# A seven-product step at the head of three matrix calls in a feed-forward layer

## The chip, the cores and the metric

The kernel runs on one core of a Trainium2 chip. The metric is the time of one execution on the device, in microseconds (us); the median of a few runs is given. The engines are TensorE (PE; its weight loads are shown as PEld), VectorE (DVE), ScalarE (ACT), GpSimd (POOL) and SyncE (SP, which here only issues DMAs). Everything is in float32.

## The reference

Two layers over 256 tokens of width 2048, each a mixer and a feed-forward part, with a normalisation before each and a last one behind:

```python
def rms_norm(x, g):
    y = x * lax.rsqrt(jnp.mean(x * x, axis=-1, keepdims=True) + EPS)
    return y * g

def sq_relu_mlp(h, w1, w2):          # w1: 2048 x 8192, w2: 8192 x 2048
    return jnp.square(jax.nn.relu(h @ w1)) @ w2

def reference(x, ...):
    x = x + neighbourhood_attention(rms_norm(x, na_norm), na_wqkv, na_rpb, na_wo)
    x = x + sq_relu_mlp(rms_norm(x, ffn0_norm), ffn0_w1, ffn0_w2)
    x = x + dilated_attention(rms_norm(x, dil_norm), dil_wqkv, dil_wo)
    x = x + sq_relu_mlp(rms_norm(x, ffn1_norm), ffn1_w1, ffn1_w2)
    return rms_norm(x, final_norm)
```

The change lies in `sq_relu_mlp`, at its first matrix, w1 ("first matrices" of the two layers).

## The kernel before

**Matrix products in parts.** A float32 operand is kept as a rounded part (hi, type float32r) and the residue (lo). A product is three matmuls: hi·hi, hi·lo, lo·hi (`three`, L199 to L201), each 128 x 128 against 128 x 512. ScalarE casts to hi and VectorE subtracts for lo (`split`, L194 and L195: `wh` and `wl` for the weights).

**The feed-forward part** works in four groups of 2048 hidden columns. Each group has four calls of `gemm_pair`: two with w1 (`cp` 0 and 1, 1024 columns each), then two with w2. A call makes a block of 256 x 1024 results: 2 x 2 blocks of 128 tokens x 512 columns. It has eight steps, one for each "pair", 256 rows of the weights: a 2 x 2 block product of 2 x 2 blocks. A plain step ("s") does eight products, 24 matmuls. An "x" step does the same work with seven products of sums of blocks (the Strassen-Winograd scheme), 21 matmuls: it needs sums of the activations' blocks (S1 to S4, made once: `sums_and_parts`) and sums of the weights' blocks (made in each step: `prep_x`). With w1 pairs 2, 4 and 6 are "x" in each call (`FF_PAIRS`), so the steps are s s x s x s x s; with w2 the order is s s x s x s x s too, except in the last group.

**Banks.** All eight banks of PSUM are one tile. A call uses four for the plain blocks, called "2", "4", "S" and "3", and four for the extra products, "1", "6", "7", "5". Call by call they change places (`sum_banks`): the banks of "1", "6", "7", "5" are those in which the call before had "2", "4", "S", "3", and the other way round. A plain step's products come in the order "2", "4", "S", "3" (two products in each); a seven-product step's in the order of `X`: "1", "2", "6", "7", "4", "3", "5".

At the end of a call its banks are emptied, in the course of its last step: `begin` (L350 and after: the banks "1", "6", "7", "5" become C, a copy on ScalarE and three instructions on VectorE), then, for w2, `put` adds each of "2", "4", "S", "3" to x, one after each quarter of the step; for w1, `last_sum`. A part of C is added to x some steps later (`early`). After a call with w1 the results are transposed into spare banks in the second step of the next call.

**The order of the work is written out by hand.** The main loop goes through the steps. In step i TensorE gets the step's products in four quarters. Between them the loop issues, in this order within a quarter: transposes, what hangs on the quarter (`s.after`: begin, put, last_sum, sums of activations), and then a part of `prep(i + 2, n)`, which makes the weights' parts for the step after next. At its end stand `prep(i + 2, 3)` and `load(i + 5)`, the weights' DMA on SP. Each engine works through its queue in that order. `prep` of a plain step is two splits of half a tile (128 x 1024). `prep_x` is: three adds on VectorE (a fourth sum among them) at n = 0; a split of one half and the cast of the sums (`hs`, L180) at n = 1; the residue of the sums (`ls`) at n = 2; a split of the other half at n = 3. Four halves have buffers (`hlpool`, 4), the sums one (`sums`), their parts two (`hs`, `ls`), the weights three (`wpool`).

**The norm** ahead of a feed-forward part (`Norm`) transposes x block by block into spare banks and makes hi and lo of the activations. Of a pair in `FF_PAIRS` it keeps S1 in the place of the block A21, and S3, S2, S4 in a tile of its own (`xs`).

Of the kernel before, what the change touches and what calls it, by code (L numbers as in the profile page):

```python
# [48 lines left out]
def tile_encoder(ctx: ExitStack, tc: tile.TileContext, ins, out):  # L49
# [41 lines left out]
    def scratch(shape, name):  # L91

        if part.name[0] == "f":
            return part.pool.tile(shape, F32, name=name, tag="t", bufs=2)
        return part.pool.tile(shape, F32, name=name, tag="p", bufs=5)

    class Banks:
# [36 lines left out]
    def subtract(engine, out, a, b):  # L134
        engine.tensor_tensor(out=out, in0=a, in1=b, op=ALU.subtract)  # L135
# [156 lines left out]
    def gemm_pair(w, cp, A, sums_of, order, finish, split_end=False, soon=False):  # L292
        made, q = [], {}
        first_x = [n for n, o in enumerate(order) if o[0] == "x"]
        touched = set()

        def left(pair, which):

            t, u = A[pair // 2], 2 * (pair % 2)
            if which in ("S2", "S3", "S4"):  # L300
                c = sums_of[pair]
                return [c[:, h, ("S3", "S2", "S4").index(which), :] for h in range(2)]
            a, ts_ = {"A11": (0, 0), "A12": (1, 0), "S1": (0, 1), "A21": (0, 1), "A22": (1, 1)}[which]
            return [t[:, u + a, h, ts_ * P:(ts_ + 1) * P] for h in range(2)]

        def product(bank, a, b, last):
            if not q:
                q.update({k: banks[:, n, :] for k, n in sum_banks().items()})
            three(q[bank], a, b, bank not in touched, last)
            touched.add(bank)  # L310

        X = (("1", "A11", 2), ("2", "A12", 3), ("6", "S2", 6), ("7", "S3", 4), ("4", "A22", 0), ("3", "S4", 1),
             ("5", "S1", 5))

        for n, (kind, pair) in enumerate(order):
            k, u = pair // 2, pair % 2
            loads = [(w[k, 2 * cp + c].rearrange("p (a n) -> p a n", n=512)[:, 2 * u:2 * u + 2, :],
                      2 - 2 * c, 4 - 2 * c) for c in (1, 0)]
            if kind == "x":
                def quarter(s, m, pair=pair, n=n):  # L320
                    for bank, a, b in X[2 * m:2 * m + 2]:
                        product(bank, left(pair, a), (s.hi[b], s.lo[b]), n == first_x[-1] and bank in "1567")
            else:
                def quarter(s, m, pair=pair, n=n):
                    tb, c = QUARTERS[m]
                    for kk in range(2):
                        b = 2 * (1 - c) + kk
                        a = (("A11", "A12"), ("A21", "A22"))[tb][kk]
                        product(STD[tb, c], left(pair, a), (s.hi[b], s.lo[b]), n == len(order) - 1 and kk == 1)
            s = Step(kind, loads, quarter)  # L330
            s.even = pair % 2 == 0
            steps.append(s)
            made.append(s)

        if split_end:
            ends = made[-2:]
            for e, s in enumerate(ends):
                def quarter(s, m, e=e):
                    tb, m = m // 2, m % 2
                    pair = order[len(order) - 2 + m][1]  # L340
                    for kk in range(2):
                        b = 2 * (1 - e) + kk
                        a = (("A11", "A12"), ("A21", "A22"))[tb][kk]
                        product(STD[tb, e], left(pair, a), (ends[m].hi[b], ends[m].lo[b]), m == 1 and kk == 1)
                s.quarters = quarter

        def begin(m):
            if m == 0:
                C = q["C"] = part.pool.tile([P, 4, 512], F32, name="C", tag="C")
                nc.scalar.copy(C[:, 0, :], q["1"])  # L350
                subtract(nc.vector, C[:, 1, :], q["6"], C[:, 0, :])
            elif m == 1:
                subtract(nc.vector, q["C"][:, 2, :], q["C"][:, 1, :], q["7"])
            elif m == 2:
                add(nc.vector, q["C"][:, 1::2, :], q["C"][:, 1:3, :], q["5"].unsqueeze(1).to_broadcast([P, 2, 512]))

        s = made[first_x[-1] + 1]
        for m in range(3):
            s.after[0 if s is made[-1] else min(m, 1) if soon else m].append(lambda m=m: begin(m))
        finish(made, q)  # L360
        return made
# [8 lines left out]


    class Norm:
        def __init__(self, n, perm, pairs=()):
            self.n, self.perm = n, perm
            self.pairs, self.sums = pairs, {}
            self.xT = [None] * NB
            self.ss = small.tile([P, 2, NB], F32, name="ss", tag="ss", bufs=2)
# [14 lines left out]
        def parts(self, c, half):  # L392
# [1 line left out]
                self.xT[c] = xpool.tile([P, 4, 2, T], F32R, name="xT", tag="xT")  # L394
            xT = self.xT[c]
            if 2 * c + half in self.pairs:
                raw = scratch([P, 2, T], "gx")
                for a in range(2):
                    k = 4 * c + 2 * half + a
                    nc.scalar.activation(raw[:, a, :], self.tp[:, a, :], AF.Copy, scale=gT[:, self.n, k:k + 1])  # L400
                self.sums[2 * c + half] = part.pool.tile([P, 2, 3, P], F32R, name="xs", tag="xs", bufs=len(self.pairs))
                sums_and_parts(raw, xT, half, self.sums[2 * c + half])
                return
            for which, a in [(which, 2 * half + a) for which in ("hi", "lo") for a in range(2)]:
# [46 lines left out]
            self.r = small.tile([P, 2], F32, name="rstd", tag="rstd", bufs=2)  # L451
            nc.vector.tensor_copy(self.r, self.r_ps[:, 0, 0:4].rearrange("p (t u) -> p t u", u=2)[:, :, 0])

    def sums_and_parts(raw, t, half, sums):

        c = scratch([P, 3, P], "c")
        a11, a21, a12, a22 = raw[:, 0, :P], raw[:, 0, P:], raw[:, 1, :P], raw[:, 1, P:]
        subtract(nc.vector, c[:, 0, :], a11, a21)
        subtract(nc.vector, a21, a21, a22)
        subtract(nc.vector, c[:, 1, :], a11, a21)  # L460
        subtract(nc.vector, c[:, 2, :], a12, c[:, 1, :])
        hi, lo = (t[:, 2 * half:2 * half + 2, h, :] for h in range(2))
        nc.scalar.copy(hi, raw)
        nc.scalar.copy(sums[:, 0], c)
        subtract(nc.vector, lo, raw, hi.bitcast(F32))
        subtract(nc.vector, sums[:, 1], c, sums[:, 0].bitcast(F32))

    def rsqrt_mean(ss):

# [188 lines left out]
    def out_rows(w, xT, nk, norm, chunk_done, order, late_block=None):  # L658
        accs = [{} for _ in range(NB)]
        for c, k in order:  # L660
            made = gemm_rows(w, c * 512, xT, [k], accs[c], 0, nk - 1)
            if k == nk - 1:
                add_rows(made, c, accs[c], norm, chunk_done, late_block)

    def begin_norm(n, perm, pairs=()):
        norms[n] = Norm(n, perm, pairs)
        return pending_norm(lambda: norms[n], n == 2)

    FF_PAIRS = (2, 4, 6)

    def ff_order(pairs, order=range(8)):
        return [("x" if k in pairs else "s", k) for k in order]

    parts = {len(steps) + 9: "feed-forward"}
    out_rows(ins["na_wo"], na_oT, 4, lambda: norms[1], begin_norm(1, False, FF_PAIRS),
             [(c, k) for c in range(3) for k in range(3)] + [(c, 3) for c in range(3)] + [(3, k) for k in range(4)], 2)


    def ffn(norm, w1, w2, next_norm, next_done):
        for g in range(4):  # L680
# [4 lines left out]
            def hidden(made, q, cp, hT=hT, sums=sums, pairs2=pairs2, last=last):  # L685
# [14 lines left out]
                for r in range(4):  # L700
# [10 lines left out]
                    def post(r=r, held=held):  # L711
                        c, half, pair = 2 * cp + r // 2, r % 2, 4 * cp + r
                        if half == 0:
                            hT[c] = opool.tile([P, 4, 2, T], F32R, name="hT", tag="o")
                        if pair in pairs2:
                            raw = part.pool.tile([P, 2, T], F32, name="h", tag="h", bufs=2)
                            nc.scalar.copy(raw, held["t"])
# [9 lines left out]
                    at(i + 1, pe, post, quarter=r)  # L727

            for cp in range(2):
                gemm_pair(w1, 2 * g + cp, norm.xT, norm.sums, ff_order(FF_PAIRS), lambda made, q, cp=cp: hidden(made, q, cp))  # L730

            w2g = w2[4 * g:4 * (g + 1)]

# [188 lines left out]
    for hh in range(2):  # L922
# [16 lines left out]
        for h in range(4):  # L939
# [2 lines left out]
               quarter=(1, 3)[h % 2])  # L942

    parts[len(steps) + 2] = "feed-forward"
    out_rows(ins["dil_wo"], dil_oT, 2, lambda: norms[3], begin_norm(3, False, FF_PAIRS),
             [(0, 0), (1, 0), (0, 1), (1, 1), (2, 0), (2, 1), (3, 0), (3, 1)])


# [210 lines left out]
```

## Time and profile before

| | |
|---|---|
| median of 3 runs | 2255.3 us (2255.12 to 2255.54) |
| the profiled execution | 2256.32 us |
| its span, first to last instruction | 2254.5 us |
| mean granted TensorE clock | 0.998 |
| first feed-forward part, its steps | 398.6 to about 1081 us |
| second feed-forward part | 1562.6 to about 2240 us |
| first steps of groups two to four | 569.95, 739.67, 909.37 and 1733.91, 1903.60, 2073.30 us |

How its lines are read: a row of the timeline is "start, duration, engine, line, operation, output <- inputs, shapes, count [idle time before it <- what ended it]". The durations of consecutive instructions of VectorE overlap a little, so that the spacing of their starts is the time they take in the queue: a 128 x 1024 residue has 1.22 us and takes 1.14. A row of the waits is "who <- for whom: us in total, times, longest". A row of the windows is "stretch, its length, busy time (and count) of PE, PEld, DVE, ACT and POOL, granted clock, busy share of the DMA engines, GB/s". A row of the groups of instructions ends in "busy us, mean ns of one | idle before".

### The profile page before, as it was taken

What the parts mean: (1) busy time and instruction counts of PE and PEld (TensorE: products, weight loads), DVE (VectorE), ACT (ScalarE), POOL (GpSimd) and SP (SyncE); (2) the same over time, 40 slices, a digit from 0 to 9 for tenths busy, and PEclk for the clock granted to TensorE, in tenths of its full rate; (3) what the DMA queues carried; (4) which work ended last, traced back from release to release, by engine and by line L of the source; (5) the groups of instructions that cost most, each with busy time, mean ns of one, the idle gap of its engine ahead of it and who ended that gap; (6) DMA issues with size and microseconds to landing.
All of it is one profiled execution on the core that took longest, in us unless ns stands there. A gap on an engine that the chain in (4) does not pass through costs nothing.

```text
span 2254.5 us, 28417 instructions
## 1 busy us (share of the span) xinstructions
PE 2241.5 (99%) x10924; PEld 1888.4 (84%) x10924; DVE 1871.7 (83%) x2215; ACT 1261.0 (56%) x1570; POOL 0.7 (0%) x6
## 2 busy tenths in 40 slices
PE   9999999999999999999999999999999999999998
PEld 8888888888888888888888888888888888888886
DVE  6776666899899999989877667757999999999988
ACT  6454455665565565565544544456665665665664
POOL 0000000000000000000000000000000000000000
PEclk9999999999999999999999999999999999999999
DMA  7556555556656656655555445444666666666664
GB/s 250 180 183 197 174 180 180 190 187 206 204 187 204 205 189 200 204 180 189 211 182 184 174 168 181 175 168 150 207 206 194 197 203 195 200 193 202 203 216 138
DMA packets 110728, 430.33 MB, mean 191 GB/s; under 512 B 23872, under 2 KB 24448, under 8 KB 92160
## 3 DMA queue, kind: packets, MB, share of 16 engines
q1 hardware_dynamic: 109920, 426.82, 57.9%
q8 instruction: 85, 1.39, 0.2%
q10 hardware_dynamic: 672, 1.70, 0.2%
q14 instruction: 51, 0.42, 0.1%
HBM read 426.38 MB, written 2.10 MB: 190 GB/s over the span
## 4 chain that ended last, share of the span: by engine, by line
PE 97%; DVE 1%; ACT 1%; issue 1%; DMA 0%; ACTq 0%; POOLq 0%; POOL 0%; DVEq 0%
PE banks L200 25%; PE banks L201 25%; PE banks L199 25%; PE banks L228 13%; PE banks L233 7%; PE banks L708 1%; PE banks L390 0%; DMA w<-in_na_wqkv_dram 0%; PE banks L906 0%; PE banks L866 0%; PE banks L603 0%; ACT junk L382 0%; DVE wl L195 0%; ACT wh L194 0%; DVE sums L138 0%
## 5 line engine op out<-in xcount | busy, mean ns | idle before, releaser
L195 DVE TENSOR_TENSOR wl<-w,wh 128x1024 fp32r<-128x1024 f32 (+1 forms) x802 | 965.1, 1218 | 254.4 <-ACT wh L194 165.9
L194 ACT CAST wh<-w 128x1024 fp32r<-128x1024 f32 (+1 forms) x802 | 828.2, 1048 | 496.4 <-PE banks L201 338.2
L199 PE MATMUL banks<-wh,xT 128*128 128x512 f32 x1104 | 434.9, 394 | 0.0
L200 PE MATMUL banks<-wl,xT 128*128 128x512 f32 x1104 | 430.1, 390 | 0.5 <-DVE wl L195 0.5
L201 PE MATMUL banks<-wh,xT 128*128 128x512 f32 x1104 | 430.1, 390 | 0.0
L199 PE MATMUL banks<-wh,hT 128*128 128x512 f32 x804 | 316.2, 393 | 0.0
L228 PE MATMUL banks<-xT,wh 128*128 128x512 f32 x1280 | 312.8, 393 | 1.1 <-DVE xT L421 1.1
L201 PE MATMUL banks<-wh,hT 128*128 128x512 f32 x804 | 313.2, 390 | 0.0
L200 PE MATMUL banks<-wl,hT 128*128 128x512 f32 x804 | 312.9, 389 | 0.0
L228 PEld LDWEIGHTS banks<-xT,wh 128*128 128x128 f32 x1280 | 233.4, 189 | 46.2 <-DVE xT L421 1.3
L201 PEld LDWEIGHTS banks<-wh,xT 128*128 128x128 f32 x1104 | 207.3, 188 | 43.5
L200 PEld LDWEIGHTS banks<-wl,xT 128*128 128x128 f32 x1104 | 207.6, 188 | 41.9 <-DVE wl L195 1.4
L199 PEld LDWEIGHTS banks<-wh,xT 128*128 128x128 f32 x1104 | 207.5, 188 | 40.8
L180 ACT CAST hs<-sums 128x1536 fp32r<-128x1536 f32 x92 | 136.4, 1483 | 159.9 <-DVE sums L138 159.9
L201 PEld LDWEIGHTS banks<-wh,hT 128*128 128x128 f32 x804 | 150.9, 188 | 31.7
L199 PEld LDWEIGHTS banks<-wh,hT 128*128 128x128 f32 x804 | 151.0, 188 | 30.1
L200 PEld LDWEIGHTS banks<-wl,hT 128*128 128x128 f32 x804 | 151.1, 188 | 30.0
L233 PE MATMUL banks<-xT,wl 128*128 128x256 f32 x1280 | 172.7, 284 | 0.0
L233 PEld LDWEIGHTS banks<-xT,wl 128*128 128x128 f32 x1280 | 165.8, 191 | 6.4 <-DVE wl L195 0.2
L135 DVE TENSOR_TENSOR ls<-sums,hs 128x1536 fp32r<-128x1536 f32 x92 | 161.2, 1752 | 10.7 <-ACT hs L180 10.7
L138 DVE TENSOR_TENSOR sums<-w 128x1024 f32<-128x1024 f32 x92 | 112.1, 1219 | 0.0
L199 PE MATMUL banks<-wh,oT 128*128 128x512 f32 x192 | 76.6, 399 | 0.0
(190 smaller groups left out, 2298.2 us busy)
## 6 DMA issues: line engine op xcount, KB each, us to landing
w<-in_ffn_w_dram SPq DMA_DIRECT2D x512, 512.0 KB, 4.7
w<-in_dil_wqkv_dram SPq DMA_DIRECT2D x72, 1024.0 KB, 4.8
w<-in_na_wqkv_dram SPq DMA_DIRECT2D x47, 1024.0 KB, 5.1
w<-in_na_wo_dram SPq DMA_DIRECT2D x16, 1024.0 KB, 4.8
w<-in_dil_wo_dram SPq DMA_DIRECT2D x8, 1024.0 KB, 4.8
bias<-in_rpb_dram SPq DMA_DIRECT2D x32, 96.0 KB, 9.9
out_dram<-x SPq DMA_DIRECT2D x8, 256.0 KB, 2.6
x<-in_x_dram SPq DMA_DIRECT2D x3, 512.0 KB, 9.3
```

What stands on the lines that cost most here:

```text
L135: engine.tensor_tensor(out=out, in0=a, in1=b, op=ALU.subtract)
L138: engine.tensor_tensor(out=out, in0=a, in1=b, op=ALU.add)
L180: nc.scalar.copy(s.hs, s.sums)
L194: nc.scalar.copy(dst_hi, src)
L195: nc.vector.tensor_tensor(out=dst_lo, in0=src, in1=dst_hi.bitcast(F32), op=ALU.subtract)
L199: nc.tensor.matmul(o, left[0], right[0], start=start, stop=False)
L200: nc.tensor.matmul(o, left[0], right[1], start=False, stop=False)
L201: nc.tensor.matmul(o, left[1], right[0], start=False, stop=stop)
L228: nc.tensor.matmul(acc[j // 2][:, j % 2, :], s.hi[a][:, j * P:(j + 1) * P], xT[k][:, a].rearrange("p h t -> p (h t)"), start=k == 0 and a ...
L233: nc.tensor.matmul(acc[j // 2][:, j % 2, :T], s.lo[a][:, j * P:(j + 1) * P], xT[k][:, a, 0, :], start=False, stop=k == nk - 1 and a == 3)
L708: nc.tensor.transpose(t[:, a, tb * P:(tb + 1) * P], q["C"][:, 2 * tb + f // 4, f % 4 * P:(f % 4 + 1) * P], ident)
```

## The change

In groups two to four the first call with w1 has pair 0 as a seven-product step too: x s x s x s x s. The second call with w1, and group one, keep pair 0 plain; so for pair 0 the norm keeps A21 and makes four sums (`FF_KEPT`, tile `xk`). With this the sums are made in a tile of seven blocks (`blocks`: three sums, four own blocks), in which two of the four small subtractions are one instruction, and the norms' scratch tiles share its two buffers ("h").

```diff
     def scratch(shape, name):
         if part.name[0] == "f":
-            return part.pool.tile(shape, F32, name=name, tag="t", bufs=2)
+            return part.pool.tile(shape, F32, name=name, tag="h", bufs=2)
...
-            if which in ("S2", "S3", "S4"):
+            names = ("S3", "S2", "S4", "S1")[:sums_of[pair].shape[2]] if pair in sums_of else ()
+            if which in names:
                 c = sums_of[pair]
-                return [c[:, h, ("S3", "S2", "S4").index(which), :] for h in range(2)]
+                return [c[:, h, names.index(which), :] for h in range(2)]
...
             if 2 * c + half in self.pairs:
-                raw = scratch([P, 2, T], "gx")
+                keep = int(2 * c + half in self.kept)
+                raw = blocks()
...
-    def sums_and_parts(raw, t, half, sums):
-
-        c = scratch([P, 3, P], "c")
-        a11, a21, a12, a22 = raw[:, 0, :P], raw[:, 0, P:], raw[:, 1, :P], raw[:, 1, P:]
-        subtract(nc.vector, c[:, 0, :], a11, a21)
-        subtract(nc.vector, a21, a21, a22)
-        subtract(nc.vector, c[:, 1, :], a11, a21)
-        subtract(nc.vector, c[:, 2, :], a12, c[:, 1, :])
-        hi, lo = (t[:, 2 * half:2 * half + 2, h, :] for h in range(2))
-        nc.scalar.copy(hi, raw)
-        nc.scalar.copy(sums[:, 0], c)
-        subtract(nc.vector, lo, raw, hi.bitcast(F32))
-        subtract(nc.vector, sums[:, 1], c, sums[:, 0].bitcast(F32))
+    def blocks():
+        return part.pool.tile([P, 7, P], F32, name="h", tag="h", bufs=2)
+
+    def sums_and_parts(b, t, half, sums):
+        hi, lo = (t[:, 2 * half:2 * half + 2, h, :].rearrange("p a (u t) -> p a u t", u=2) for h in range(2))
+        whole = b[:, 3:7, :].rearrange("p (a u) t -> p a u t", u=2)
+        keep = sums.shape[2] == 4
+        def own():
+            nc.scalar.copy(hi, whole)
+            subtract(nc.vector, lo, whole, hi.bitcast(F32))
+        if keep:
+            own()
+        subtract(nc.vector, b[:, 0:5:4, :], b[:, 3:5, :], b[:, 4:7:2, :])
+        subtract(nc.vector, b[:, 1, :], b[:, 3, :], b[:, 4, :])
+        subtract(nc.vector, b[:, 2, :], b[:, 5, :], b[:, 1, :])
+        if not keep:
+            nc.scalar.copy(hi, whole)
+        for n, src in ((slice(0, 3), b[:, 0:3, :]), (slice(3, 4), b[:, 4:5, :]))[:1 + keep]:
+            nc.scalar.copy(sums[:, 0, n], src)
+        if not keep:
+            subtract(nc.vector, lo, whole, hi.bitcast(F32))
+        for n, src in ((slice(0, 3), b[:, 0:3, :]), (slice(3, 4), b[:, 4:5, :]))[:1 + keep]:
+            subtract(nc.vector, sums[:, 1, n], src, sums[:, 0, n].bitcast(F32))
...
-    FF_PAIRS = (2, 4, 6)
+    FF_PAIRS, FF_KEPT = (2, 4, 6), (0,)
...
             for cp in range(2):
-                gemm_pair(w1, 2 * g + cp, norm.xT, norm.sums, ff_order(FF_PAIRS), lambda made, q, cp=cp: hidden(made, q, cp))
+                gemm_pair(w1, 2 * g + cp, norm.xT, norm.sums, ff_order(FF_PAIRS + (FF_KEPT if g and not cp else ())), lambda made, q, cp=cp: hidden(made, q, cp))
```

More of the change, by code (lines that the diff above doesn't have):

```diff
@@ L372, in tile_encoder, with __init__ @@
     class Norm:
-        def __init__(self, n, perm, pairs=()):
-            self.n, self.perm = n, perm
+        def __init__(self, n, perm, pairs=(), kept=()):
+            self.n, self.perm, self.kept = n, perm, kept
             self.pairs, self.sums = pairs, {}
@@ L396, in parts @@
             if 2 * c + half in self.pairs:
-                raw = scratch([P, 2, T], "gx")
+                keep = int(2 * c + half in self.kept)
+                raw = blocks()
                 for a in range(2):
                     k = 4 * c + 2 * half + a
-                    nc.scalar.activation(raw[:, a, :], self.tp[:, a, :], AF.Copy, scale=gT[:, self.n, k:k + 1])
-                self.sums[2 * c + half] = part.pool.tile([P, 2, 3, P], F32R, name="xs", tag="xs", bufs=len(self.pairs))
+                    nc.scalar.activation(raw[:, 3 + 2 * a:5 + 2 * a, :].rearrange("p u t -> p (u t)"), self.tp[:, a, :], AF.Copy, scale=gT[:, self.n, k:k + 1])
+                self.sums[2 * c + half] = part.pool.tile([P, 2, 3 + keep, P], F32R, name="xs", tag=("xs", "xk")[keep],
+                                                              bufs=1 if keep else len(self.pairs) - len(self.kept))
                 sums_and_parts(raw, xT, half, self.sums[2 * c + half])
@@ L663, in out_rows, with begin_norm @@
                 add_rows(made, c, accs[c], norm, chunk_done, late_block)
-    def begin_norm(n, perm, pairs=()):
-        norms[n] = Norm(n, perm, pairs)
+    def begin_norm(n, perm, pairs=(), kept=()):
+        norms[n] = Norm(n, perm, pairs + kept, kept)
         return pending_norm(lambda: norms[n], n == 2)
-    FF_PAIRS = (2, 4, 6)
+    FF_PAIRS, FF_KEPT = (2, 4, 6), (0,)
     def ff_order(pairs, order=range(8)):
@@ L674, in tile_encoder @@
     parts = {len(steps) + 9: "feed-forward"}
-    out_rows(ins["na_wo"], na_oT, 4, lambda: norms[1], begin_norm(1, False, FF_PAIRS),
+    out_rows(ins["na_wo"], na_oT, 4, lambda: norms[1], begin_norm(1, False, FF_PAIRS, FF_KEPT),
              [(c, k) for c in range(3) for k in range(3)] + [(c, 3) for c in range(3)] + [(3, k) for k in range(4)], 2)
@@ L715, in post @@
                         if pair in pairs2:
-                            raw = part.pool.tile([P, 2, T], F32, name="h", tag="h", bufs=2)
-                            nc.scalar.copy(raw, held["t"])
+                            raw = blocks()
+                            nc.scalar.copy(raw[:, 3:7, :].rearrange("p (a u) t -> p a (u t)", u=2), held["t"])
                             def parts_of(c=c, half=half, raw=raw, pair=pair):
@@ L944, in tile_encoder @@
     parts[len(steps) + 2] = "feed-forward"
-    out_rows(ins["dil_wo"], dil_oT, 2, lambda: norms[3], begin_norm(3, False, FF_PAIRS),
+    out_rows(ins["dil_wo"], dil_oT, 2, lambda: norms[3], begin_norm(3, False, FF_PAIRS, FF_KEPT),
              [(0, 0), (1, 0), (0, 1), (1, 1), (2, 0), (2, 1), (3, 0), (3, 1)])
```

## The prediction

> **What bounds the kernel now.** I read the page first: the span, the engines' busy time, and the chain that ended last.
>
> ```profile
> span 2254.5 us, 28417 instructions
> PE 2241.5 (99%) x10924; PEld 1888.4 (84%) x10924; DVE 1871.7 (83%) x2215; ACT 1261.0 (56%) x1570; POOL 0.7 (0%) x6
> ...
> PE 97%; DVE 1%; ACT 1%; issue 1%; DMA 0%; ACTq 0%; POOLq 0%; POOL 0%; DVEq 0%
> ```
>
> TensorE sets the end: 97% of the chain. A matmul taken away counts in full, as long as nothing makes TensorE wait. So next the waits, and then the busy times over one whole group of the first feed-forward layer (group two, 569.95 to 739.67 us).
>
> ```profile
> ACT wh L194 <- PE banks L201: 338.2, 253, 3.2
> PEld banks L200 <- DVE wl L195: 1.4, 2, 0.7
> PEld banks L199 <- DVE hT L195: 1.3, 8, 0.2
> ...
> 569.95:739.67 169.72, 169.72 (x766) 140.52 (x764) 158.40 (x170) 101.22 (x110) 0.00 (x0) 1.00 0.62 199
> ```
>
> ScalarE's casts wait for TensorE (338.2 us, for a free buffer), while TensorE's own waits in the feed-forward part are of the order of 1 us in all. One of them matters here: eight times a weight load waited for VectorE to empty a bank (hT L195). In the group TensorE is busy for all of its 169.72 us, but VectorE for 158.40 of them, 93%. It has 11 us to spare per group, and where in the group they lie decides this case.
>
> The price of the two kinds of step is read from TensorE's timeline at the border between group one and group two (the first matmuls of the last two steps of group one, and of the first step of group two).
>
> ```profile
> 559.75 0.39 PE L199 MATMUL banks<-wh,hT 128*128 128x512 f32 x1
> ...
> 564.51 0.39 PE L199 MATMUL banks<-wh,hT 128*128 128x512 f32 x1
> ...
> 569.95 0.39 PE L199 MATMUL banks<-wh,xT 128*128 128x512 f32 x1
> ...
> 569.72 0.19 PEld L199 LDWEIGHTS banks<-wh,xT 128*128 128x128 f32 x1
> ```
>
> A step of seven products takes 564.51 - 559.75 = 4.76 us (21 matmuls), one of eight 569.95 - 564.51 = 5.44 us (24 matmuls): 0.227 us a matmul. The first weight load of the step that the change turns into seven products starts at 569.72.
>
> **The change part by part.**
>
> *TensorE.* Six steps (three groups in two layers) go from 24 to 21 matmuls: 6 x 0.68 = 4.1 us less.
>
> *VectorE and ScalarE at the border.* The new step, called x0 here, needs sums of weights: it is prepared like other seven-product steps. Its preparation is issued during the step of 559.75, ahead of the emptying of that call's banks. VectorE's and ScalarE's queues there:
>
> ```profile
> 550.88 1.23 DVE L195 TENSOR_TENSOR wl<-w,wh 128x1024 fp32r<-128x1024 f32 x1 [0.18 <-ACT wh L194]
> 552.02 1.22 DVE L138 TENSOR_TENSOR sums<-w 128x1024 f32<-128x1024 f32 x1
> 553.28 0.69 DVE L138 TENSOR_TENSOR sums<-sums,w 128x512 f32<-128x512 f32 x1
> 554.00 0.69 DVE L138 TENSOR_TENSOR w<-sums,w 128x512 f32<-128x512 f32 x1
> 554.61 1.22 DVE L195 TENSOR_TENSOR wl<-w,wh 128x1024 fp32r<-128x1024 f32 x1
> 555.75 1.75 DVE L135 TENSOR_TENSOR ls<-sums,hs 128x1536 fp32r<-128x1536 f32 x1
> 557.42 1.22 DVE L195 TENSOR_TENSOR wl<-w,wh 128x1024 fp32r<-128x1024 f32 x1
> 558.55 0.68 DVE L135 TENSOR_TENSOR x<-x,C 128x512 f32<-128x512 f32 x1
> ...
> 559.75 3.87 DVE L195 TENSOR_TENSOR wl<-w,wh 128x1024 fp32r<-128x1024 f32 x3
> 565.11 1.23 DVE L195 TENSOR_TENSOR wl<-w,wh 128x1024 fp32r<-128x1024 f32 x1 [1.49 <-ACT wh L194]
> 566.26 0.68 DVE L135 TENSOR_TENSOR C<-banks,C 128x512 f32<-128x512 f32 x1
> ...
> 568.90 1.28 DVE L138 TENSOR_TENSOR x<-x,banks 128x512 f32<-128x512 f32 x2
> 570.10 1.22 DVE L195 TENSOR_TENSOR wl<-w,wh 128x1024 fp32r<-128x1024 f32 x1
> 571.23 1.28 DVE L138 TENSOR_TENSOR x<-x,banks 128x512 f32<-128x512 f32 x2
> 572.43 1.22 DVE L195 TENSOR_TENSOR wl<-w,wh 128x1024 fp32r<-128x1024 f32 x1
> ```
>
> ```profile
> 559.99 1.05 ACT L194 CAST wh<-w 128x1024 fp32r<-128x1024 f32 x1 [1.66 <-PE banks L201]
> 561.31 1.06 ACT L194 CAST wh<-w 128x1024 fp32r<-128x1024 f32 x1 [0.26 <-PE banks L201]
> 564.03 1.05 ACT L194 CAST wh<-w 128x1024 fp32r<-128x1024 f32 x1 [1.66 <-PE banks L201]
> 564.98 0.58 ACT L350 COPY C<-banks 128x512 f32<-128x512 f32 x1
> ```
>
> From 552.02 to 558.55 VectorE prepares the step of 559.75: three adds, two residues of halves (wl), one of the sums (ls), 6.53 us by spacing. An eight-product step needs only two halves, 2 x 1.14 = 2.28 us. The three wl from 559.75 are two for the step of 564.51 and one for today's first step of group two, whose second half is at 565.11, after 1.49 us idle. From 566.26 come the sums of the banks of the call that ends (begin, L350 on); at 568.90 the first two banks that hold blocks of the result are added to x (put), at 571.23 the other two, with a residue for the next step between.
>
> After the change, VectorE's queue: the second wl of 559.75 waits for the cast that ends at 561.04, and with its 1.14 us VectorE is free at about 562.2. This instant is pinned by TensorE's release of a weight buffer (1.66 <-PE), so savings earlier in the queue don't move it. Then x0's preparation takes 6.53 us, to 568.73. ScalarE is not in its way: the cast of x0's first half is the one at 561.31, the cast of the sums can start near 564.2, and the second half's buffer is free at 564.0. begin's first subtraction starts at 568.73, not 566.26: 2.47 us later. The first put ends at 568.90 + 0.68 + 2.47 = 572.05, the third at 571.23 + 0.68 + 2.47 = 574.38.
>
> *Who waits for that.* An eight-product step opens with the four banks "2", "4", "S", "3", which lie where the last call had "1", "6", "7", "5", empty early in begin. x0 opens with product "1", and sum_banks puts "1", "6", "7", "5" where the last call had "2", "4", "S", "3": the banks that the four puts empty. So x0's first matmul waits for the first put, "6" for the second, "7" for the third, "5" for the fourth. How fast TensorE resumes is shown by one of the eight waits:
>
> ```profile
> 624.70 0.68 DVE L195 TENSOR_TENSOR hT<-banks,hT 128x512 fp32r<-128x512 f32 x1
> ...
> 625.44 0.19 PEld L199 LDWEIGHTS banks<-hs,xs 128*128 128x128 f32 x1 [0.16 <-DVE hT L195]
> ```
>
> The evacuation ends at 625.38 and the load starts at 625.44: 0.06 us. So x0's first load starts at 572.11 instead of 569.72: 2.39 us of waiting. Product "7" comes nine matmuls on, at 574.15, and its bank is ready at 574.44: 0.29 us more. "6" (bank ready at 572.7, due at 573.5) and "5" (ready at 575.0, due at 576.5) don't wait. The border costs 2.39 + 0.29 - 0.68 = +2.0 us, and six of them +12.0 us. The bounds: if the first matmul and not its weight load waits, 0.23 us less each; if the two bubbles of 1.49 and 0.18 us hid another 0.5, +1.2 a border; if casts hold VectorE up for 0.6, +2.6. So +7 to +16 us.
>
> Behind the wait: VectorE is then 2.47 us late and TensorE 2.0, which leaves later steps 0.5 us less lead. The next seven-product step has its residues 3 us ahead, so I cost that at nothing. Weight loads issued when a preparation ends go out some 2.5 us later on SP, for a step whose preparation is ten us off: nothing, unless VectorE is asked for them sooner.
>
> *The norms before the feed-forward parts.* Pair 0 gets a raw copy, own parts and four sums instead of two scaled casts and residues.
>
> ```profile
> 368.36 1.75 DVE L421 SCALAR_TENSOR_TENSOR xT<-banks,gT,xT 128x256 fp32r<-128x256 f32 x4
> ...
> 374.70 0.28 DVE L135 TENSOR_TENSOR c<-gx 128x128 f32<-128x128 f32 x1
> ...
> 378.15 1.28 DVE L487 TENSOR_TENSOR x<-x,banks 128x512 f32<-128x512 f32 x2
> ...
> 385.97 2.36 DVE L195 TENSOR_TENSOR wl<-w,wh 128x1024 fp32r<-128x1024 f32 x2
> ...
> 390.67 0.39 PE L200 MATMUL banks<-wl,oT 128*128 128x512 f32 x1
> ```
>
> A block with a summed pair takes VectorE 378.15 - 374.70 = 3.45 us, a plain one 1.75: +1.7 us, and some 0.6 us for the fourth sum. The tightest residue afterwards ends at 387.2 and is used at 390.67: 3.5 us of cover. I take 0; if ScalarE and VectorE wait for each other there and the delay doubles, up to +1.
>
> *Merged subtractions.* Each of 28 calls has three small subtractions for four.
>
> ```profile
> L135 DVE TENSOR_TENSOR h<-h 128x128 f32<-128x128 f32 x22 | 6.4, 292 | 0.8
> ```
>
> That is under 0.3 us of VectorE a call, and only where TensorE waits for a residue does it count: the 1.4 us in two waits above, at each layer's first seven-product step. I take 2 x 0.26 = -0.5 us; between 0 and -1.4.
>
> **Sum.** The profiled execution took 2256.3 us (its span and 1.8 around it); 2256.3 + 12.0 - 0.5 = 2267.8. The median of the runs is 1.0 lower than this execution, so 2266.8 us. By the bounds 2261 to 2272.
>
> **The rivals.** *No wait, faster.* VectorE has room on average: 158.40 + 6.53 - 2.28 in 169.72 - 0.68 is 96%. If the queue's slack let the puts end in time, only TensorE's saving is left: 2255.3 - 4.1 - 0.5 = 2250.7 us. It decides at one point: the border breaks even when the first wait is 0.39 us, so when the first put ends at 570.05, 2.0 us before my place for it; the 562.2 against it is pinned by a cast. The Trainium skill, "Perfetto Trace Analysis", section "Identifying the Most-Contended Engine", takes occupancy as a fair measure of how near VectorE is to its limit; by that rule 96% still fits and this rival's time comes out. I hold the order of the queue against it: in the 14 us from 558.55 there are 2 us of idle time, and they are not ahead of the puts by enough.
>
> *A part of the wait.* With a first wait of 0.4 to 1.1 us the change moves the time by less than 0.2% (4.5 us, about what a measurement of this kernel can tell from no change).
>
> *The lag carries on.* If the 0.5 us of lost lead, an early() on VectorE and the seven-product steps two on add another wait of 0.5 to 1.2 us per border: 2266.8 + 3 to 7, 2270 to 2274 us.
>
> *The clock falls.* A TensorE that stands still for 2.4 us could be granted less clock. The one idle stretch like it is the end of the program:
>
> ```profile
> 2239.00:2255.00 16.00, 5.54 (x25) 4.26 (x23) 7.32 (x19) 5.62 (x14) 0.00 (x0) 0.73 0.35 132
> ```
>
> There, with some 10 us of idle TensorE, the mean clock is 0.73; in the group's row it is 1.00. Half clock through x0 would cost up to 4.76 us a border, 2295 us at most. The Trainium skill, "TensorE: Matmul & The Clock Gate", section "What's actually happening", has the clock halved after an idle window of about 3.4 us; by that rule 2.4 us are too short, and no run here shows such a wait yet.
>
> **How the numbers follow.** The bank wait as worked out 0.76 (2266.8; its own range 2261 to 2272); carried on 0.07; clock 0.03; a part of it 0.07; no wait 0.07. Slower 0.86, same 0.07, faster 0.07. The range, 2260 to 2274, takes in the first two, 0.83.
>
> **What would show it.** In the profile after: 18 matmuls fewer on L199 to L201's successors; a weight load of wh, xT that waited for VectorE's x six times, some 2.4 us each; x0 about 7.4 us from its first matmul's due time to the next step's, not 4.76; begin's first subtraction 2.5 us later against the step before. The prediction is wrong if those waits are under 0.7 us, if VectorE's sums of x0 start before 562, or if TensorE's new idle time lies elsewhere, in the norms above all.

## The result and the profile after

The changed kernel takes 2275.9 us (median of five runs, 2273.5 to 2277.1) against 2255.3 (2254.9 to 2255.5) for the kernel before: slower by 20.6 us, a ratio of 1.0089 (95% interval 1.0077 to 1.0100). The forecast was slower by 11.5, with a range up to 2274. The sign and the main mechanism came out; some 9 us more were lost in two places that the forecast held to cost nothing.

The page of the profile after, span and engines:

```profile
span 2274.1 us, 28388 instructions
PE 2246.6 (99%) x10906; PEld 1888.3 (83%) x10906; DVE 1895.6 (83%) x2219; ACT 1271.1 (56%) x1582; POOL 0.7 (0%) x6
```

There are 10906 matmuls for 10924, the 18 that were to go. The span is 19.6 us longer. The waits of the kernel after ("who <- for whom: us in total, times, longest"), those of TensorE that are new or longer:

```profile
PEld banks L199 <- ACT wh L194: 15.1, 6, 2.5
PE banks L199 <- DVE x L138: 12.7, 6, 2.1
PEld banks L391 <- ACT wh L194: 3.0, 2, 1.5
PE banks L391 <- DVE x L504: 2.7, 4, 1.1
```

The first two rows are one event at each of the six borders, told by two queues. The weight load was followed back to a cast of ScalarE that had long been done; the matmul's own row names what came last: VectorE's addition of a bank to x, the put. The last two rows are the norms: L391 is the transposes of x, and they wait for VectorE's additions to x too.

The border in the timeline of VectorE and of TensorE, kernel after, to be read beside the rows of the kernel before in the prediction:

```profile
562.82 1.22 DVE L138 TENSOR_TENSOR sums<-w 128x1024 f32<-128x1024 f32 x1
...
568.21 1.22 DVE L195 TENSOR_TENSOR wl<-w,wh 128x1024 fp32r<-128x1024 f32 x1
569.34 0.69 DVE L135 TENSOR_TENSOR C<-banks,C 128x512 f32<-128x512 f32 x1
...
571.99 1.28 DVE L138 TENSOR_TENSOR x<-x,banks 128x512 f32<-128x512 f32 x2
573.19 1.22 DVE L195 TENSOR_TENSOR wl<-w,wh 128x1024 fp32r<-128x1024 f32 x1
574.32 1.28 DVE L138 TENSOR_TENSOR x<-x,banks 128x512 f32<-128x512 f32 x2
```

```profile
570.31 0.39 PE L201 MATMUL banks<-wh,hT 128*128 128x512 f32 x1
572.82 0.47 PE L199 MATMUL banks<-wh,xT 128*128 128x512 f32 x1 [2.12 <-DVE x L138]
...
579.31 0.39 PE L199 MATMUL banks<-wh,xT 128*128 128x512 f32 x1
```

VectorE makes x0's sums and residues from 562.82 to 569.34 (6.52 us by spacing), begin follows, and the puts start at 571.99. x0's first matmul, due at 570.54 (570.31 and a spacing of 0.23), runs at 572.82: late by 2.28, of which 2.12 is shown as idle. So far this is the forecast. But from 572.82 to the next step's first matmul at 579.31 lie 6.49 us, not some 5.1: x0 itself is slow. The reason is in the windows (stretch, length, busy time and count of PE, PEld, DVE, ACT, POOL, granted clock, DMA share, GB/s). Three borders, each with the stretch of the wait and the one behind it; at the second and third also the one ahead of them, in which the wait begins:

```profile
570.08:573.49 3.41, 1.29 (x6) 0.81 (x5) 3.31 (x5) 1.04 (x1) 0.00 (x0) 1.00 0.83 247
573.49:576.91 3.42, 3.42 (x10) 2.63 (x9) 3.42 (x5) 1.05 (x1) 0.00 (x0) 0.50 0.16 65
740.75:744.16 3.41, 2.98 (x14) 2.13 (x12) 3.27 (x5) 1.40 (x2) 0.00 (x0) 1.00 0.15 31
744.16:747.57 3.41, 1.72 (x8) 1.47 (x9) 3.41 (x5) 0.78 (x2) 0.00 (x0) 1.00 0.80 281
747.57:750.98 3.41, 3.41 (x16) 2.53 (x15) 3.38 (x5) 0.98 (x1) 0.00 (x0) 1.00 0.12 13
1914.94:1918.35 3.41, 3.15 (x14) 2.26 (x13) 3.27 (x5) 1.39 (x3) 0.00 (x0) 1.00 0.18 19
1918.35:1921.76 3.41, 1.55 (x7) 1.32 (x8) 3.41 (x5) 0.87 (x1) 0.00 (x0) 1.00 0.83 291
1921.76:1925.17 3.41, 3.41 (x16) 2.56 (x15) 3.41 (x5) 1.05 (x1) 0.00 (x0) 1.00 0.02 1
```

At the first border the granted clock is 0.50 in the stretch behind the wait, and 10 matmuls go where 16 go at full clock. This happens at four of the six borders. The falls start at 573.49, 918.24, 1747.68 and 2092.43 and last 3.41 us each; the starts lie whole multiples of 3.4133 us apart (344.75 is 101 of them, 829.44 is 243), so in this profile the clock is granted in pieces of a fixed grid. In the piece ahead of each fall TensorE stood still for 2.11 to 2.12 us of 3.41. At the other two borders the wait was as long, but the grid cut it in two: 0.43 us in one piece and 1.69 in the next (from 740.75), or 0.26 and 1.86 (from 1914.94), and no fall came. At these two x0 takes 5.10 us, with weights loaded and prepared in the same way.

**The account** of the 19.6 us, from matmul to matmul in the two profiles:

| part | us |
|---|---|
| six borders: first wait 2.28, a second (product "7") 0.34, three matmuls fewer 0.68: 1.94 each | +11.6 |
| four falls of the clock: x0 takes 6.44 to 6.50 instead of 5.10, 1.37 each on average | +5.5 |
| the two norms (from the first matmul with oT to the first transposes of hidden columns: 147.4 for 145.6, and 104.6 for 102.8) | +3.7 |
| the start of the program, up to the first matmul with oT: untouched by the change, and different from profile to profile | -1.2 |

At the four borders with a fall the parting of the first two rows is one of bookkeeping: there x0 takes 6.47 us on average, 1.71 more than the 4.76 of a step without a wait, which is half of 3.41. TensorE is then so slow that product "7" no longer waits (its weight load waits for a put at the two other borders alone); its 0.34 is booked in the first row, the rest in the second.

### The profile page after: what moved, and what is told of

It is laid out like the page before. It is cut to its first block, busy times and chain, and to the rows that moved or that the text cites. A ratio compares the mean times of both kernels' runs of the same rounds, so it can differ in the third digit from the quotient of the medians.

```text
span 2274.1 us, 28388 instructions
## 1 busy us (share of the span) xinstructions
PE 2246.6 (99%) x10906; PEld 1888.3 (83%) x10906; DVE 1895.6 (83%) x2219; ACT 1271.1 (56%) x1582; POOL 0.7 (0%) x6
## 4 chain that ended last, share of the span: by engine, by line
PE 94%; DVE 3%; ACT 1%; issue 1%; ACTq 0%; POOLq 0%; DVEq 0%; POOL 0%
PE banks L199 24%; PE banks L201 24%; PE banks L200 24%; PE banks L228 13%; PE banks L233 7%; PE banks L725 1%; DVE wl L195 1%; DVE sums L138 1%; DVE ls L135 1%; PE banks L391 0%; ACT wh L194 0%; DVE C L135 0%; PE banks L923 0%; PE banks L883 0%; PE banks L620 0%
## 5 line engine op out<-in xcount | busy, mean ns | idle before, releaser
L199 PE MATMUL banks<-wh,xT 128*128 128x512 f32 x1074 | 424.7, 395 | 12.7 <-DVE x L138 12.7
L201 PE MATMUL banks<-wh,xT 128*128 128x512 f32 x1074 | 420.1, 391 | 0.0
L200 PE MATMUL banks<-wl,xT 128*128 128x512 f32 x1074 | 419.6, 391 | 0.5 <-DVE wl L195 0.5
L199 PE MATMUL banks<-wh,hT 128*128 128x512 f32 x804 | 316.2, 393 | 0.0
L199 PEld LDWEIGHTS banks<-wh,xT 128*128 128x128 f32 x1074 | 202.0, 188 | 54.6 <-ACT wh L194 15.1
L180 ACT CAST hs<-sums 128x1536 fp32r<-128x1536 f32 x98 | 145.3, 1483 | 176.5 <-DVE sums L138 176.5
L201 PEld LDWEIGHTS banks<-wh,xT 128*128 128x128 f32 x1074 | 202.2, 188 | 42.5
L200 PEld LDWEIGHTS banks<-wl,xT 128*128 128x128 f32 x1074 | 202.5, 189 | 40.9 <-DVE wl L195 1.4
L135 DVE TENSOR_TENSOR ls<-sums,hs 128x1536 fp32r<-128x1536 f32 x98 | 171.7, 1752 | 12.5 <-ACT hs L180 12.5
L199 PEld LDWEIGHTS banks<-wh,hT 128*128 128x128 f32 x804 | 151.0, 188 | 30.2
L138 DVE TENSOR_TENSOR sums<-w 128x1024 f32<-128x1024 f32 x98 | 119.4, 1218 | 0.0
L199 PE MATMUL banks<-wh,oT 128*128 128x512 f32 x192 | 76.6, 399 | 0.0
```

What stands on the lines that cost most here:

```text
L138: engine.tensor_tensor(out=out, in0=a, in1=b, op=ALU.add)
L180: nc.scalar.copy(s.hs, s.sums)
L199: nc.tensor.matmul(o, left[0], right[0], start=start, stop=False)
L200: nc.tensor.matmul(o, left[0], right[1], start=False, stop=False)
L201: nc.tensor.matmul(o, left[1], right[0], start=False, stop=stop)
```

## The experiments

The theory after the result: (A) the borders lose 1.9 us each because x0's first product goes to the bank that is emptied last; (B) some waits also cost a fall of the clock, 1.4 us, if they stand within one piece of the grid; (C) the norms lose 1.5 to 1.8 us each through the order of VectorE's queue. Rivals: x0's slowness is not the clock but the DMA traffic or late weights; the loss is VectorE's load and not the order of banks; the norms' part is scatter. Differences are medians against the kernel before on the same chip, each with the ratio and its 95% interval.

**Without the x0 steps** (norms and subtractions of the change kept).

```diff
-... ff_order(FF_PAIRS + (FF_KEPT if g and not cp else ())) ...
+... ff_order(FF_PAIRS) ...
```

> The changed kernel with pair 0 plain in every call: no border step of seven products, but the norms still make four sums for pair 0 and the subtractions are merged. Theory (the loss is made at the six borders, by waits for VectorE's puts and the clock that falls on them; the norms cost 1.33 us each, where transposes wait for VectorE's additions to x): all the border waits go, no fall of the clock, two waits of 1.3 us at the transposes stay: 2255.3 + 2.7 = 2258.0 us. Rival (the fall of the clock and the loss come from the norms or from the new tiles, and not from the borders): above 2265 us. Rival (the 1.33 us are made good later): 2255.3 us.

+3.0 us (1.0014, 1.0005 to 1.0024). In its waits no matmul of L199 waits for x, and the two rows of the norms stand as in the changed kernel:

```profile
PEld banks L391 <- ACT wh L194: 3.0, 2, 1.5
PE banks L391 <- DVE x L504: 2.7, 4, 1.1
```

So the norms' preparation of pair 0 costs some 3 us whether its sums are used or not (by the interval 1 to 5; the two norms take 147.4 and 104.7 us here, as in the changed kernel).

**The merged subtractions alone** (as above, and the norms keep no fourth sum):

```diff
-... begin_norm(1, False, FF_PAIRS, FF_KEPT) ...
+... begin_norm(1, False, FF_PAIRS) ...
```

and the same for the norm of the second layer.

> Merged subtractions alone: pair 0 plain in every call and without sums in the norms. Theory: VectorE saves some 7 us in all, but not where TensorE waits: 2255.3 us, within 0.5. The prediction's term for it was -0.5 us, so 2254.8. Rival (the shared scratch buffers cost): over 2256.5.

0.0 us (1.0001, 0.9991 to 1.0010). The form of the subtractions is worth nothing that can be measured; the 3 us lie in pair 0's sums.

**The wait filled with matmuls.** Ten matmuls whose product the next one overwrites run ahead of x0's first product, so that TensorE is late but hardly stands still:

```diff
+if n == 0 and m == 0:
+    q.update({k: banks[:, v, :] for k, v in sum_banks().items()})
+    for _ in range(10):
+        nc.tensor.matmul(q["2"], left(pair, "A11")[0], s.hi[2], start=True, stop=True)
```

> The changed kernel with ten matmuls more at the head of each of the six new steps, 10 x 0.227 = 2.27 us, into a bank that is free and is started anew afterwards: TensorE works through what was its wait. Theory (the clock falls because TensorE stands still, and a fall costs 1.4 us): the border takes as long as with the wait, but the clock stays at 1.00, so 2255.3 + 6 x (2.28 + 0.34 - 0.68) + 2.7 = 2269.6 us, against 2275.9 of the changed kernel. Rival (the falls come from the steps themselves or from elsewhere): three to five falls as before, 2275 us. Rival (the wait is on something that the matmuls push back): 2283 us.

+15.4 us (1.0067, 1.0050 to 1.0084). The window over the first border, then the waits:

```profile
566.00:584.00 18.00, 18.00 (x80) 14.46 (x79) 17.79 (x19) 9.33 (x9) 0.00 (x0) 1.00 0.53 167
```

```profile
PEld banks L199 <- DVE x L138: 3.6, 12, 0.4
```

TensorE does 2.3 us of thrown-away work per border and still ends some 5 us earlier than the changed kernel. The clock stays at 1.00 at all six borders. There x0 with the ten takes 7.37 to 7.41 us, which is 2.27 for the ten and 5.10 to 5.14 for x0. The weights are loaded and prepared at the same places of the program as in the changed kernel, so it is not they that make x0 slow: standing still does.

**A longer wait.** VectorE makes one residue of x0 twice, 1.14 us more ahead of the puts:

```diff
         if s.border:
+            subtract(nc.vector, lo, w[:, 0:2, :], hi.bitcast(F32))
```

(`border` marks the first step of groups two to four, here and below.)

> The changed kernel with one VectorE subtraction of 128 x 1024 more (1.14 us) ahead of each of the six bank sums: it doubles nothing but the lateness of the puts. Theory (TensorE's wait at the border is the lateness of the puts): the first wait grows from 2.1 to 3.3 us standing still, 6 x 1.14 = 6.8 us: 2269.6 + 6.8 = 2276.4 us without clock falls; with a fall wherever more than about six tenths of a 3.41 us stretch on a fixed grid stands still, some five of the six borders, 1.4 us each or a little more: 2283 to 2286 us. Rival (the clock needs a whole idle stretch of 3.4 us, as the Trainium skill has it): no border, or nearly none, falls, 2276 to 2278 us. Rival (the wait is not on the puts): no change, 2276 us with the same falls.

+30.6 us (1.0136, 1.0121 to 1.0151). Its waits, and its windows at two borders:

```profile
PE banks L202 <- DVE x L139: 20.3, 6, 3.4
```

```profile
571.83:575.24 3.41, 1.28 (x6) 1.10 (x7) 3.31 (x5) 0.00 (x0) 0.00 (x0) 1.00 0.88 298
575.25:578.65 3.40, 3.40 (x10) 2.63 (x9) 3.40 (x5) 1.04 (x1) 0.00 (x0) 0.50 0.01 2
1749.43:1752.84 3.41, 0.77 (x4) 0.31 (x2) 3.27 (x5) 1.04 (x1) 0.00 (x0) 1.00 0.41 80
1752.85:1756.25 3.40, 2.67 (x6) 2.15 (x7) 3.40 (x5) 0.00 (x0) 0.00 (x0) 0.50 0.57 225
1756.26:1759.66 3.40, 3.40 (x9) 2.64 (x8) 3.33 (x5) 1.31 (x2) 0.00 (x0) 0.50 0.25 55
```

With 3.4 us of wait the clock falls at all six borders, where the grid cut none of the waits small enough, and once for two pieces. 20.3 - 12.7 = 7.6 us more of waits and three more pieces of half clock (two borders more, and the second piece) at 1.4 make 11.8; the two profiled executions stand 11.0 us apart in their spans (2285.1 and 2274.1), the differences above 10 us (30.6 and 20.6).

**The same wait in two pieces.** x0's last residue and the weights' load behind it are issued behind the first two puts, in the second quarter of the step before x0, and no longer ahead of begin:

```diff
+if n == 1 and i + 1 < len(steps) and steps[i + 1].border:
+    prep(i + 1, 3)
+    load(i + 4)
...
-prep(i + 2, 3)
-load(i + 5)
+if not (i + 2 < len(steps) and steps[i + 2].border):
+    prep(i + 2, 3)
+    load(i + 5)
```

> The changed kernel with the last residue of the new step (1.14 us of VectorE) issued behind the first two puts instead of ahead of the bank sums; the third and fourth put stay where they were. Theory (each of the products waits for its own put): the first wait shrinks from 2.1 to about 1.0 us standing still, and the one ahead of product 7 grows from 0.34 to 1.48, so the border takes as long as with one wait, 1.94 us over before; but no 3.41 us stretch stands still for more than half, so no fall of the clock: 14 to 15.4 us over before, as with the filled wait (15.35). Rival (what counts is the first put alone): 6 x 1.14 us less, 7 to 8.5 us over before. Rival (the clock counts waits, or falls by chance): 18 to 21 us over before.

+16.0 us (1.0069, 1.0052 to 1.0086), and the waits:

```profile
PE banks L200 <- DVE x L139: 12.6, 12, 1.1
```

The total stands as in the changed kernel, 12.6 us for 12.7, but in twelve waits of 1.05. No piece of half clock is left at a border, and 4.6 us are gone. This parts (B) from every explanation by the sum of the waits.

**Another order of x0's products.** "2", "4" and "3" go to banks that are empty early; x0 now starts with them, so far as the sums allow:

```diff
+X0 = [X[n] for n in (1, 4, 5, 0, 2, 3, 6)]
...
-for bank, a, b in X[2 * m:2 * m + 2]:
+for bank, a, b in (X if n else X0)[2 * m:2 * m + 2]:
```

> The changed kernel with another order of the seven products in the six new steps: 2, 4, 3, 1, 6, 7, 5, so that those come first whose banks are emptied by the bank sums and not by the puts. No instruction of VectorE or ScalarE moves. Theory (the order of the banks makes the wait): product 3 waits 0.47 us for the last bank sum, product 7 0.88 us for the third put, in all 1.35 - 0.68 = 0.67 us a border, no fall of the clock; with the 3.0 us of the norms 7.0 us over before. Rival (VectorE is too full, whatever the order): 15 to 20 us over before.

+7.8 us (1.0033, 1.0021 to 1.0045). Waits:

```profile
PEld banks L199 <- DVE x L138: 6.1, 6, 1.0
PEld banks L199 <- DVE C L138: 2.9, 6, 0.5
```

VectorE's work is the same, and 13 of 20.6 us are gone, 5.5 of them the falls of the clock, which no longer come. It is the order of the banks (A). What is left at each border: two waits of weight loads, 0.5 us for begin and 1.0 for a put; in the matmuls x0 takes 6.02 us, 1.26 more than without a wait.

**That order, and the puts sooner.** In the step before x0, three quarters of the next step's preparation move behind the puts:

```diff
-elif i and n < 3:
+elif i and n < 3 and not (i + 1 < len(steps) and steps[i + 1].border):
     prep(i + 2, n)
...
+if i + 1 < len(steps) and steps[i + 1].border:
+    for n in range(3):
+        prep(i + 2, n)
```

> As the kernel with the other order of the products, and the residue of the next plain step's first half (1.14 us) issued behind the four puts instead of between them. Theory: product 7 no longer waits; 0.47 - 0.68 = -0.2 us a border, and 3.0 us of the norms: 1.7 us over before. Rival (the plain step behind then waits for its residue, up to 1.1 us a border): 8 us over before.

+2.3 us (1.0009, 1.0000 to 1.0018). One wait a border is left:

```profile
PEld banks L200 <- DVE C L139: 2.9, 6, 0.5
```

x0 takes 5.12 us, 0.36 more than without a wait and 0.32 less than the plain step; the first feed-forward part is 0.9 us shorter than before and the second as well. The norms' 3 us make it a loss.

**VectorE's load alone.** Steps plain as before, but at the borders three sums, their cast and residue are made and thrown away, 4.2 us of VectorE each. In a first version (`extra` ahead of the step's own preparation) ScalarE cast the sums ahead of the first half:

```diff
         s = steps[i]
+        if s.border:
+            extra(s, n)
```

> The changed kernel with pair 0 plain in every call, but with VectorE and ScalarE doing at the six borders what a step of seven products needs (three additions, a cast and a residue of sums of weights, thrown away), so that the puts come as late as in the changed kernel. Theory (it is the order in which the banks are needed, not VectorE's load): a plain step opens with the banks that are empty early; no wait, no fall of the clock, 3.0 us over before as without this work. Rival (VectorE is too full at the border): six waits of some 2 us, 15 us over before or more.

+15.3 us (1.0067, 1.0052 to 1.0082), five times what was expected. VectorE's timeline says why:

```profile
568.74 1.23 DVE L213 TENSOR_TENSOR wl<-w,wh 128x1024 fp32r<-128x1024 f32 x1 [2.50 <-ACT wh L212]
...
572.69 0.69 DVE L136 TENSOR_TENSOR C<-banks,C 128x512 f32<-128x512 f32 x1
```

VectorE stood 2.50 us for a cast that now came behind the sums' cast, so begin started 3.3 us later than in the changed kernel. This is a delay that the change does not have, so the run does not decide between the theory and its rival; it does show that a plain step waits too when begin is that late (its weight loads waited for begin six times, 1.0 us each). In a second version `extra` follows the half's split:

> As the kernel with the thrown-away work at the borders and plain steps, but with the cast of the sums behind the cast of the first half, as in a real step of seven products (in the kernel before it stood ahead of it, ScalarE's next casts queued behind it, and the puts came 3.3 us later still than in the changed kernel, with waits of 0.6 us for the bank sums). Now the puts are as late as in the changed kernel, 2.5 us later than before. Theory (it is the order in which the banks are needed): no wait at the border, no fall of the clock, 3.0 us over before. Rival (VectorE's load makes the wait): 12 us over before or more.

+3.9 us (1.0017, 1.0008 to 1.0026), with the norms' 3.0 in it. VectorE, and TensorE at the border:

```profile
570.14 0.69 DVE L136 TENSOR_TENSOR C<-banks,C 128x512 f32<-128x512 f32 x1
...
572.79 1.28 DVE L139 TENSOR_TENSOR x<-x,banks 128x512 f32<-128x512 f32 x2
```

```profile
570.60 0.39 PE L219 MATMUL banks<-wh,hT 128*128 128x512 f32 x1
570.83 0.39 PE L217 MATMUL banks<-wh,xT 128*128 128x512 f32 x1
```

begin starts 0.69 us ahead of the step's first matmul, in the changed kernel 1.20 ahead of its due time; the first put starts at 572.79, two microseconds after that matmul. A plain step does not mind: it opens with the banks that begin empties, and takes its 5.44 us at all six borders. A VectorE as late as in the changed kernel costs nothing by itself.

**The norms' sums later.** Pair 0's own parts are made at once, its sums at the end of the step; no x0 steps:

```diff
+                if keep:
+                    own_parts(raw, xT, half)
+                    f = lambda c=c: sums_and_parts(raw, xT, half, self.sums[2 * c + half])
+                    steps[now["i"]].evac.append(f)
```

> As the kernel with pair 0 plain and sums for it in the norms, but with the making of pair 0's sums issued behind the next step's additions to x instead of ahead of them (the same instructions, later in the queue). Theory (the transposes of the next block wait for those additions, which stood behind the sums): the two waits of 1.33 us go, and the 3.0 us over before with them: 0 to 0.5 us over before. Rival (the extra work itself costs): 2.5 to 3 us over before.

+2.2 us (1.0011, 1.0002 to 1.0020): 0.8 less than without the x0 steps alone, where 2.5 to 3 were expected; by the two intervals that difference alone is not clear of noise, so the trace has to decide. Its waits and the first layer's norm on TensorE:

```profile
PE banks L391 <- DVE x L510: 1.5, 2, 1.3
```

```profile
382.20 0.30 PE L391 MATMUL banks<-ident,x 128*128 128x128 f32 x1 [1.29 <-DVE x L510]
```

In the second layer the wait went: its norm takes 103.2 us instead of 104.7 (102.8 before). In the first, which stays at 147.6, it moved to the next block of transposes, 1.29 us at 382.20, whose x is added at 381.37, behind the same sums. So (C) is shown as a matter of the queue's order; an order that frees both layers was not found.

**Two tries at a faster kernel.** The order of products with puts sooner and the norms' sums later, x0 steps in place:

> The kernel with the products in the order 2, 4, 3, 1, 6, 7, 5 and the next step's residue behind the puts, with pair 0's sums in the norms later as well. It ran 2.3 us over before with the norms as they were. Theory: 2.7 to 3.0 us of that go: 0.4 to 0.7 us faster than before, which the measurement can hardly tell from no change. Rival: it stays over before.

+0.8 us (1.0004, 0.9995 to 1.0013), where 0.4 to 0.7 us less than before was expected: no change that can be measured. And with begin moved ahead, to the end of the step before the call's last, two parts of x0's preparation moved behind the puts, and the order "2", "1", "4", "3", "6", "7", "5":

> A version for gain: the six steps of seven products, with the bank sums issued right behind the three additions of weights, then the first half's residue, the first two puts, the second half's residue, the residue of the sums, the last two puts, and the next step's residues last; the products in the order 2, 1, 4, 3, 6, 7, 5; pair 0's sums in the norms later. Worked out along VectorE's queue each product finds its bank and its residues but for some 0.2 us at product 7. Theory: 0.2 - 0.68 = -0.5 us a border, six times, and nothing for the norms: 2.5 to 3.0 us faster than before (0.1%). Rival (a residue or a cast comes too late in the new order, by 0.5 us or more a border): no faster than before.

+0.9 us (1.0003, 0.9995 to 1.0012), where -2.5 to -3.0 was expected. TensorE's weight loads at the first border:

```profile
573.40 0.19 PEld L201 LDWEIGHTS banks<-ls,xs 128*128 128x128 f32 x1 [0.17 <-DVE ls L136]
...
574.00 0.19 PEld L200 LDWEIGHTS banks<-hs,xs 128*128 128x128 f32 x1 [0.30 <-DVE x L139]
...
575.73 0.19 PEld L201 LDWEIGHTS banks<-wl,xT 128*128 128x128 f32 x1 [0.28 <-DVE wl L196]
```

Three short waits of the loads, 0.75 us, for a residue of the sums, a put and, in the step behind x0, a residue of a half. In the matmuls they cost less: x0 takes 4.95 us instead of 4.76 and the step behind it 5.59 instead of 5.44, 0.34 together, half of the 0.68 saved. The two feed-forward parts are 1.0 and 0.5 us shorter than before, and the two norms 2.0 and 0.4 us longer. So in the orders tried late work of VectorE takes back half or more of what x0 saves, and the norms the rest. None of the versions beats the kernel before by a measurable amount.

## Why the prediction was right in direction and short in size

Two terms failed that the prediction put at nothing in its sum: the fall of the clock (+5.5 us in the profile) and the norms (+3.0 us by the run without x0 steps, +3.7 in the profile). The border, its largest term, was sized rightly.

**Right: the border.** "x0's first matmul waits for the first put": late by 2.28 us, forecast 2.39. "begin's first subtraction 2.5 us later": its lead on the border's first due matmul is 1.20 us (569.34 against 570.54), before 3.69 (566.26 against 569.95): 2.49 less. Product "7" waits too, 0.34 for 0.29. Together with 0.68 saved that is +11.6 against the forecast +12.0. The other order of products, with the same work on VectorE, took most of it away, and the load without x0 did not bring it: the step of the argument that goes from the banks' places to the wait is shown. The rival "no wait" is refuted by six waits of 2.1 us, and with it the reading of 96% as room enough: by its occupancy VectorE had time, but not in that order. "The lag carries on" isn't seen either: the steps behind x0 keep their length (5.44 us at all six borders). "x0 about 7.4 us from its first matmul's due time to the next step's" holds at the two borders without a fall (7.38); at the four others it is 8.7 to 8.8, and that is the next point.

**Wrong first: the clock.** The rival "the clock falls" had 0.03, on the ground that "by that rule 2.4 us are too short, and no run here shows such a wait yet". The Trainium skill, "TensorE: Matmul & The Clock Gate", section "What's actually happening", speaks of an idle window of about 3.4 us. The length of the window agrees with the 3.41 us pieces here. That it must be idle throughout, as the prediction read it, does not: pieces with 2.11 us of standstill (62%) were followed by 0.50, pieces with 1.86 (54%) were not, and here the measurement decides. The size was off the other way: half clock lasts one piece, not all of x0, and costs 1.37 us, not "up to 4.76 a border".

The step that failed is a row used beyond what it showed: the end of the program gave a mean clock of 0.73 over 16 us, and the prediction did not ask after which stretch the clock fell. Windows of 3.41 us answer it, in the kernel before:

```profile
2243.09:2246.50 3.41, 1.45 (x7) 0.87 (x5) 2.50 (x7) 1.95 (x6) 0.00 (x0) 1.00 0.18 68
2246.50:2249.92 3.42, 0.00 (x0) 0.00 (x0) 1.90 (x6) 2.13 (x5) 0.00 (x0) 0.50 0.73 273
```

The first of them has 1.96 us of standstill, less than the 2.39 forecast at a border, and the next is at 0.50. So the kernel before already showed a fall behind a shorter standstill than the one forecast.

Four falls made +5.5 us in the profiled execution; without them its time would lie near 2270, inside the range. That it was four and not two or six is a matter of where the borders fell on the grid, which no working from the queue could give. The changed kernel's runs spread over 3.6 us, those of the kernel before over 0.6. The mean granted clock is 0.995 to 0.996 in four of the five and 0.997 in the fastest (2273.5 us). A piece at half clock takes 0.00075 off the mean, so that some two falls fewer there, 2.7 us, would fit; the falls themselves were counted only in the profiled execution.

**Wrong second: the norms.** "I take 0", with "3.5 us of cover" read from the tightest residue. The extra time on VectorE was sized about rightly, 1.7 and 0.6 us for 2.7 measured (0.9 of them waits of VectorE for ScalarE's casts), but the cover was looked for at the wrong user. Behind pair 0's sums in VectorE's queue stand the additions to x of the next block, and TensorE's transposes wait for them. The first layer, kernel before, VectorE and TensorE:

```profile
370.02 1.27 DVE L487 TENSOR_TENSOR x<-x,banks 128x512 f32<-128x512 f32 x2
```

```profile
372.28 0.60 PE L390 MATMUL banks<-ident,x 128*128 128x128 f32 x4
```

And after:

```profile
371.52 1.28 DVE L504 TENSOR_TENSOR x<-x,banks 128x512 f32<-128x512 f32 x2
```

```profile
372.35 0.30 PE L391 MATMUL banks<-ident,x 128*128 128x128 f32 x1 [1.12 <-DVE x L504]
```

The additions start 1.50 us later, and 2.7 later against the matmuls, which run 1.2 us ahead in this profile (the start of the program in the account). Before, the first of the two additions ended 1.58 us ahead of the transposes (370.02 + 0.68 for 372.28); this was the cover, and 2.7 - 1.58 is the 1.12 of idle time. After, the matmul starts a little after that addition has ended (371.52 + 0.68). Without x0 steps the norms cost +3.0 us.

**Wrong third: the merged subtractions.** Taken at -0.5, measured 0.0. The change's first seven-product steps of the two layers take 5.52 and 5.51 us, before 5.43 and 5.42: the waits there are not shorter.

## What to carry to other kernels

Ask of each buffer when it is emptied and which of the next step's operations wants it first; an engine that is busy 93% of a stage can make another wait two microseconds, and reordering the products takes most of that back at no cost. When work is put into an engine's queue, look through everything queued behind it and through who waits for each, not only at the results of the added work. A wait of TensorE can cost more than its length: here 2.1 us within one 3.41 us piece brought 1.4 us more, and the same time in two halves did not.

## What the runs showed of the hardware that was not expected

The granted clock moves on a fixed grid of 3.413 us (the starts of the falls in the changed kernel). A piece in which TensorE stood still for 2.11 us or more was followed by a piece at 0.50 each time it came at a border in the profiles of the changed kernel and of the longer wait (four and six borders); pieces with 1.86 us and less were not. At the end of the kernel before, 1.96 us was enough. Where between 1.86 and 1.96 the border of the two lies, and whether it counts time or matmuls, stays open. After a wait of 3.4 us the half clock lasted two pieces once in six; there 0.73 us of the wait lay in the first piece at half clock.
